# Expert keys of a product-key router: two one-hots over 16 ranks instead of one over 50 candidates, with the ranks stepped out on GpSimd

## The chip, the cores and the metric

The kernel runs on one core of a Trainium2 chip. The metric is the device time of one launch in microseconds. The engines are named as in the profile: PE (TensorE matmuls) and PEld (its weight loads), DVE (VectorE), ACT (ScalarE), POOL (GpSimd) and SP (SyncE, here only a queue of transfers). Each engine works through its own queue in order and waits on semaphores of the others.

## The reference, cut to what matters

Two layers, each a gated merge of four token mixers and then a PEER layer: a feed-forward layer whose 16384 experts per layer are found by product keys. 512 tokens of width 1024. The mixers are untouched by the change. What the router computes:

```python
def peer_ffn(h, w_query, sub_keys, expert_u, expert_v):
    q = (ht @ w_query).reshape(t, PEER_HEADS, 2, PEER_HALF).astype(f32)      # 8 heads, 2 halves
    sc = jnp.einsum("thpd,pkd->thpk", q, sub_keys.astype(f32))               # 128 keys per half
    s_top, i_top = lax.top_k(sc, PEER_TOPK)                                  # 16 best of each half
    cand = (s_top[:, :, 0, :, None] + s_top[:, :, 1, None, :]).reshape(t, PEER_HEADS, 256)
    best, pos = lax.top_k(cand, PEER_TOPK)                                   # 16 best pairs
    idx = (jnp.take_along_axis(i_top[:, :, 0, :], pos // PEER_TOPK, axis=-1) * PEER_KEYS
           + jnp.take_along_axis(i_top[:, :, 1, :], pos % PEER_TOPK, axis=-1))
    gate = jax.nn.softmax(best, axis=-1).astype(h.dtype)
    # then, chunk by chunk: gelu(expert_u[idx] . h) * gate, times expert_v[idx], summed
```

## The kernel before

**The work of a PEER layer.** All experts are computed densely for three of the four token tiles (384 tokens), and by gathered rows for the fourth. `up` (one call is a *block* here) multiplies 128 experts with the tokens: a block is 24 matmuls of 128x384, in three products of a split into a high and a low part. The weights of a block come by a transfer from SP (`wr`); ACT casts them (`wh`, line 108), DVE subtracts to get the low part (`wl`, line 109: the *split* below), PE multiplies. 92 blocks run in `up`, their results go to memory; the other blocks and the products with the second expert matrix follow in `Down`.

**The router** runs beside these blocks. `Router.pairs(t, R)` handles one token tile of 128 tokens: on DVE it sums the scores of the 50 rank pairs that can be among the best 16 (`cand`; the ranks of the first half from 0 to 7 have 16, 8, 5, 4, 3, 2, 2, 2 partners, ranks 8 to 15 one each: `ROWS`, `NCAND`), sums their keys in the same layout (`cidx`), takes the best 16 (`topk`, two calls of four heads), and turns the position of each winner (`posf`) into its key: per head, a one-hot of 16x50 on DVE (`eq`, line 1167), times `cidx` on POOL (line 1169), summed on DVE (line 1171). Last the key is parted into its two halves and the softmax is taken, with an Exp on ACT. `pairs` is called four times a layer: once for the gathered tile (`first`, beside blocks 2 to 12), then by `dense` for tiles 0, 1 and 2. After each of these three, `dense` transposes the result (`rT`), builds one-hots for 32 groups of four tokens (`oh`) and multiplies them on PE to a table of gates (`G`, `GB`). `gathered` gets rows of experts by indirect transfers that POOL issues (line 1251) and reduces them on DVE (`row`, line 1260), at 0.8 rows per block while `dense` runs.

**What sets the order.** The program is written out by hand. Each call of `bulk` first runs `Beside.tick`: every generator beside the blocks (`scores`, `pairs`, `dense`, `gathered`) gets a rate per block (`RF` 3.2 for the first `pairs`, `RG` 3.1 for `dense`) and goes on until the costs that it yields use that up. So a larger number at a `yield` spreads the work over more blocks. After the block's matmuls, `Stream.advance` issues the cast and the split for the block two further on. On DVE there stands therefore, block after block: the work beside, then one split. On ACT a cast stands behind the activation of the block before (line 1279), which waits for that block's matmuls. POOL holds the products of `pairs` and the indirect transfers in one queue.

The lines that matter here are 1145 to 1180 (`pairs`), 108 and 109 (`split`), 120 to 123 (the matmuls of a block) and 1251 and 1260 (`gathered`).

## Time and profile before

| | us |
|---|---|
| median of 3 runs | 4039.18 |
| lowest, highest | 4032.03, 4041.72 |
| the profiled execution | 4033.05 |
| span of its instructions | 4031.3 |
| busy: PE, PEld, DVE, ACT, POOL | 3877.6, 3363.8, 3217.4, 1477.9, 1697.8 |

The profile is of one execution. Busy time of PE is modelled, since matmuls overlap; where a weight load or a matmul stands with "<-DVE wl L109", PE had nothing to do until that split was done. Engine times in a timeline are start and duration, in us from the span's start; two instructions of DVE overlap by up to 0.1 us in it, so the distance from start to start is what an instruction costs its queue. The two layers follow each other: the blocks of `up` run from about 840 to 1345 and again from about 2840 to 3345.

### The profile page before, as it was taken

The page shows a single profiled execution, that of the slowest core. Times are in us where ns is not written, and L with a number is a line of the kernel's source. Part 1 is how long each engine was busy: PE and PEld are TensorE (multiplying, and loading weights), DVE is VectorE, ACT ScalarE, POOL GpSimd, SP SyncE. Part 2 cuts the span into 40 slices and gives each one's busy share as a digit, 9 for nine tenths or more (in the row PEclk, how much of TensorE's full clock was granted, in tenths as well). Part 3 has the DMA queues.
Part 4 walks back from the last instruction along what each step waited for, and adds up shares of the span by engine and source line. Part 5 has one row for each costly group of instructions (what it writes and reads, how often), then busy time and mean ns, then how long its engine had stood idle before and what let it go on. Part 6 is the DMA issues. An engine that isn't in the chain of part 4 may idle for free.

```text
span 4031.3 us, 56403 instructions
## 1 busy us (share of the span) xinstructions
PE 3877.6 (96%) x19994; PEld 3363.8 (83%) x19994; DVE 3217.4 (80%) x5869; ACT 1477.9 (37%) x2171; POOL 1697.8 (42%) x1566
## 2 busy tenths in 40 slices
PE   6899999999999999999988999999999999999998
PEld 5777777799999999888767777878999999998877
DVE  4667944799999777999857778448999997788997
ACT  4323233333444333333343232333344443333333
POOL 3410500024423566899743005000233326678995
PEclk9999999999999999999989999999999999999999
DMA  3322333346876899999923232333468768999997
GB/s 113 100 85 92 99 98 115 116 134 234 292 259 235 280 322 322 347 336 343 321 92 107 82 99 93 102 113 113 159 223 294 261 226 304 322 323 337 340 348 267
DMA packets 346650, 851.39 MB, mean 211 GB/s; under 512 B 43648, under 2 KB 164864, under 8 KB 342016
## 3 DMA queue, kind: packets, MB, share of 16 engines
q1 hardware_dynamic: 236048, 492.39, 36.7%
q0 software_dynamic: 74016, 272.66, 19.1%
q10 hardware_dynamic: 36304, 82.74, 5.7%
q8 instruction: 158, 2.59, 0.3%
q14 instruction: 124, 1.02, 0.1%
HBM read 754.60 MB, written 93.06 MB: 210 GB/s over the span
## 4 chain that ended last, share of the span: by engine, by line
PE 74%; DVE 13%; POOL 5%; issue 4%; DMA 3%; ACT 2%; SPq 0%; DVEq 0%; POOLq 0%; ACTq 0%
PE mm L120 14%; PE mm L123 13%; PE mm L122 13%; PE va L129 6%; PE va L132 6%; PE va L131 6%; PE G L1218 4%; DVE wl L109 3%; PE pb L120 2%; DMA as<-dS 1%; PE pb L123 1%; PE pb L122 1%; DVE row L1260 1%; DMA row<-in_v_dram,gidx 1%; POOL as L1322 1%
## 5 line engine op out<-in xcount | busy, mean ns | idle before, releaser
L109 DVE TENSOR_TENSOR wl<-wr,wh 128x1024 fp32r<-128x1024 f32 (+2 forms) x792 | 990.8, 1251 | 377.4 <-ACT wh L108 302.9
L123 PE MATMUL mm<-hl,wh 128*128 128x384 f32 (+1 forms) x3456 | 1235.9, 358 | 0.0
L122 PE MATMUL mm<-hh,wh 128*128 128x384 f32 (+1 forms) x3456 | 1235.8, 358 | 0.0
L108 ACT CAST wh<-wr 128x1024 fp32r<-128x1024 f32 (+2 forms) x792 | 789.0, 997 | 346.7 <-PE va L132 128.2
L120 PE MATMUL mm<-hh,wl 128*128 128x384 f32 (+1 forms) x3456 | 787.0, 370 | 46.2 <-DVE wl L109 42.4
L120 PEld LDWEIGHTS mm<-hh,wl 128*128 128x128 f32 x3456 | 619.8, 190 | 123.4 <-DVE wl L109 54.1
L122 PEld LDWEIGHTS mm<-hh,wh 128*128 128x128 f32 x3456 | 651.8, 189 | 56.8
L123 PEld LDWEIGHTS mm<-hl,wh 128*128 128x128 f32 x3456 | 651.1, 188 | 56.1
L1251 POOL DMA_INDIRECT row<-in_u_dram,gidx x256 | 389.4, 1521 | 611.1 <-DVE row L1260 561.7
L132 PE MATMUL va<-wh,al 128*128 128x512 f32 x1536 | 598.1, 389 | 0.8 <-DVE al L109 0.8
L131 PE MATMUL va<-wh,ah 128*128 128x512 f32 x1536 | 597.9, 389 | 0.0
L1169 POOL TENSOR_TENSOR eq<-eq,cidx 128x800 f32<-128x800 f32 x64 | 126.2, 1977 | 891.1 <-DVE eq L1167 885.4
L1251 POOL DMA_INDIRECT row<-in_v_dram,gidx x256 | 397.4, 1552 | 97.9 <-DVE gacc L1271 44.8
L1271 DVE SCALAR_TENSOR_TENSOR gacc<-row,z,gacc 128x1024 f32<-128x1024 f32 x254 | 413.3, 1627 | 20.4 <-DMA row<-in_v_dram,gidx 18.8
L129 PE MATMUL va<-wl,ah 128*128 128x512 f32 x1536 | 395.6, 392 | 7.3 <-DVE wl L109 7.2
L129 PEld LDWEIGHTS va<-wl,ah 128*128 128x128 f32 x1536 | 284.8, 188 | 70.3 <-issue 11.6
L1260 DVE SCALAR_TENSOR_TENSOR row<-row,h2row 128x1024 f32<-128x1024 f32 x256 | 339.3, 1335 | 1.6 <-DMA row<-in_u_dram,gidx 1.6
L132 PEld LDWEIGHTS va<-wh,al 128*128 128x128 f32 x1536 | 288.3, 188 | 62.2 <-DVE al L109 1.2
L131 PEld LDWEIGHTS va<-wh,ah 128*128 128x128 f32 x1536 | 288.3, 188 | 60.7
L108 ACT CAST ah<-as 128x384 fp32r<-128x384 f32 x256 | 131.0, 512 | 472.8 <-POOL as L1322 405.9
L109 DVE TENSOR_TENSOR al<-as,ah 128x384 fp32r<-128x384 f32 x256 | 173.0, 676 | 161.7 <-ACT ah L108 161.5
L1322 POOL TENSOR_TENSOR as<-as,GB 128x128 f32<-128x128 f32 x256 | 263.8, 1030 | 0.0
(345 smaller groups left out, 4331.8 us busy)
## 6 DMA issues: line engine op xcount, KB each, us to landing
wr<-in_uT_dram SPq DMA_DIRECT2D x256, 512.0 KB, 4.6
wr<-in_v_dram SPq DMA_DIRECT2D x256, 512.0 KB, 5.8
wr<-in_w_in_dram SPq DMA_DIRECT2D x144, 512.0 KB, 3.7
dS<-act ACTq DMA_DIRECT2D x184, 192.0 KB, 3.7
as<-dS SPq DMA_DIRECT2D x184, 192.0 KB, 6.7
dG<-GB ACTq DMA_DIRECT2D x32, 1024.0 KB, 6.7
ag<-dG SPq DMA_DIRECT2D x128, 256.0 KB, 6.7
wr<-in_w_query_dram SPq DMA_DIRECT2D x32, 512.0 KB, 3.7
```

Source lines behind the costliest of these rows:

```text
L108: e.nc.scalar.copy(hi, src)
L109: e.nc.vector.tensor_tensor(out=lo, in0=src, in1=hi, op=OP.subtract)
L120: e.nc.tensor.matmul(ps, al, bh, start=start and i == 0, stop=False)
L122: e.nc.tensor.matmul(ps, ah, bh, start=False, stop=False)
L123: e.nc.tensor.matmul(ps, ah, bl, start=False, stop=stop and i == n - 1)
L129: e.nc.tensor.matmul(ps, ah, bl, start=start, stop=False)
L131: e.nc.tensor.matmul(ps, ah, bh, start=False, stop=False)
L132: e.nc.tensor.matmul(ps, al, bh, start=False, stop=stop)
L1251: nc.gpsimd.indirect_dma_start(out=g, out_offset=None, in_=e.I["u" if n < 128 else "v"], in_offset=bass.IndirectOffsetOnAxis(ap=e.gidx[:, ...
L1260: V.scalar_tensor_tensor(g, g, 1.0, e.h2row, op0=OP.mult, op1=OP.mult, accum_out=z[:, k:k + 1])
L1271: V.scalar_tensor_tensor(e.gacc, g, z[:, k:k + 1], e.gacc, op0=OP.mult, op1=OP.add)
L1322: G.tensor_tensor(out=s[:, 4:6], in0=s[:, 4:6], in1=self.e.GB[:, :, (i + NS) % 128], op=OP.mult)
```

## The change

The keys of all 50 candidates (`cidx`) are no longer built. Instead, the position of a winner is turned into two ranks by 18 steps on POOL over 128x128 elements: `fo`, the first candidate of the winner's row (eight compare-and-scale steps over the row starts, added up), and `posf - fo`, the place in the row. Each rank is then looked up by a one-hot over 16 ranks for four heads at once: `eq` is now 4x16x16 = 1024 elements a partition, four of them per call instead of eight of 800, with product and sum on the same engines as before. The two halves of the key come out directly, so the parting at the end goes. The yields change with it: the lookups cost 4 x 1.2 and 2 x 2.4 times `CP` (1.4) instead of 4 x 1.0 and 6 x 1.9, the `cidx` yield of 1.2 x `CP` goes, and two yields of 2.0 stand between the 18 steps and the first one-hot. A call of `pairs` yields 28.7 in all instead of 34.5. A table of the row starts (`first`) is set up once at the start of the kernel.

```diff
@@ consts
+    e.first = p.tile([128, 16], F32, name="first")
+    for j in range(8):
+        nc.vector.memset(e.first[:, j:j + 1], float(sum(ROWS[:j])))
+    nc.vector.tensor_copy(e.first[:, 8:16], e.iota[:, NCAND - 8:NCAND])
@@ Router.pairs
-        ci = pb.tile([128, 8, NCAND], F32, name="cidx")
-        for dst, src in ((c, S1), (ci, I1)):
...
+        s = S1[:, t].rearrange("p (h q) k -> p h q k", q=2)
+        a0 = s[:, :, 0]
...
         V.tensor_copy(pf, pos)
-        idx = R[:, 3].rearrange("p (h k) -> p h k", k=16)
+        G = nc.gpsimd
+        fo, st = R[:, 0], R[:, 3]
+        pl = pf.rearrange("p h k -> p (h k)")
+        for j in range(1, 8):
+            G.tensor_scalar(st if j > 1 else fo, pl, float(sum(ROWS[:j])), float(ROWS[j - 1]), op0=OP.is_ge, op1=OP.mult)
+            if j > 1:
+                G.tensor_tensor(out=fo, in0=fo, in1=st, op=OP.add)
+        G.tensor_scalar(st, pl, float(NCAND - 8), None, op0=OP.is_ge)
+        G.tensor_scalar(R[:, 1], pl, float(sum(ROWS[:7])), None, op0=OP.subtract)
+        G.tensor_tensor(out=st, in0=st, in1=R[:, 1], op=OP.mult)
+        G.tensor_tensor(out=fo, in0=fo, in1=st, op=OP.add)
+        G.tensor_tensor(out=pl, in0=pl, in1=fo, op=OP.subtract)
+        yield 2.0
+        yield 2.0
+        rank = R[:, 0].rearrange("p (h k) -> p h k", k=16), pf
         eqs = {}
-        for h in range(10):
-            if h < 8:
-                eqs[h] = eq = self.pb.tile([128, 16, NCAND], F32, name="eq", tag="oh", bufs=OH)
-                V.tensor_tensor(out=eq, in0=bc(pf[:, h, :, None], [128, 16, NCAND]),
-                                in1=bc(e.iota[:, None, 0:NCAND], [128, 16, NCAND]), op=OP.is_equal)
-                nc.gpsimd.tensor_tensor(out=eq, in0=eq, in1=bc(ci[:, h, None, :], [128, 16, NCAND]), op=OP.mult)
-            if h > 1:
-                V.tensor_reduce(out=idx[:, h - 2], in_=eqs.pop(h - 2), axis=AX.X, op=OP.add)
-            yield (1.9 if 1 < h < 8 else 1.0) * CP
-        V.tensor_scalar(R[:, 0], R[:, 3], 1.0 / 128, -0.49609375, op0=OP.mult, op1=OP.add)
+        sh = [128, 4, 16, 16]
+        for i in range(6):
+            if i < 4:
+                q, h = i % 2, slice(i // 2 * 4, i // 2 * 4 + 4)
+                eqs[i] = eq = self.pb.tile(sh, F32, name="eq", tag="oh", bufs=OH)
+                tab = e.first if q == 0 else e.iota[:, 0:16]
+                V.tensor_tensor(out=eq, in0=bc(rank[q][:, h, :, None], sh), in1=bc(tab[:, None, None, :], sh),
+                                op=OP.is_equal)
+                key = I1[:, t].rearrange("p (h q) k -> p h q k", q=2)[:, h, q]
+                G.tensor_tensor(out=eq, in0=eq, in1=bc(key[:, :, None, :], sh), op=OP.mult)
+            if i > 1:
+                q, h = (i - 2) % 2, (i - 2) // 2 * 4
+                V.tensor_reduce(out=R[:, 1 if q else 3, h * 16:h * 16 + 64].rearrange("p (h k) -> p h k", k=16),
+                                in_=eqs.pop(i - 2), axis=AX.X, op=OP.add)
+            yield (2.4 if 1 < i < 4 else 1.2) * CP
+        V.tensor_copy(R[:, 0], R[:, 3])
...
-        V.tensor_scalar(R[:, 0], R[:, 0], 12582912.0, None, op0=OP.add)
-        V.tensor_scalar(R[:, 0], R[:, 0], 12582912.0, None, op0=OP.subtract)
-        V.scalar_tensor_tensor(R[:, 1], R[:, 0], -128.0, R[:, 3], op0=OP.mult, op1=OP.add)
+        if t == NT - 1:
+            V.scalar_tensor_tensor(R[:, 3], R[:, 0], 128.0, R[:, 1], op0=OP.mult, op1=OP.add)
```

DVE's queue in the call of `pairs` for tile 0 of layer 0, from the cast of the positions on, before the change (`wl` is a split, `row` a row of `gathered`):

```order
L1161 CAST posf<-pos 128x128
L1167 TENSOR_TENSOR eq<-posf,iota 128x800 x2
L1260 SCALAR_TENSOR_TENSOR row,z<-row,h2row 128x1024
L109 TENSOR_TENSOR wl<-wr,wh 128x1024
L1167 TENSOR_TENSOR eq<-posf,iota 128x800
L1171 TENSOR_REDUCE R<-eq 128x16
L109 TENSOR_TENSOR wl<-wr,wh 128x1024
```

The same place after the change, down to the first sum; `R` holds the first rank, `first` and `iota` are the tables it is compared with:

```order
L1161 CAST posf<-pos 128x128
L1281 SCALAR_TENSOR_TENSOR row,z<-row,h2row 128x1024
L114 TENSOR_TENSOR wl<-wr,wh 128x1024
L1281 SCALAR_TENSOR_TENSOR row,z<-row,h2row 128x1024
L114 TENSOR_TENSOR wl<-wr,wh 128x1024
L1185 TENSOR_TENSOR eq<-R,first 128x1024
L1185 TENSOR_TENSOR eq<-posf,iota 128x1024
L114 TENSOR_TENSOR wl<-wr,wh 128x1024
L1185 TENSOR_TENSOR eq<-R,first 128x1024
L1191 TENSOR_REDUCE R<-eq 128x64
L1281 SCALAR_TENSOR_TENSOR row,z<-row,h2row 128x1024
L114 TENSOR_TENSOR wl<-wr,wh 128x1024
```

Two blocks' worth of other work now stands between the cast and the first one-hot, which waits for POOL, and four splits stand beside the one-hots instead of seven. POOL's queue at that place, before:

```order
L1251 DMA row<-in_u_dram,gidx 128x1024 x5
L1169 TENSOR_TENSOR eq<-eq,cidx 128x800 x2
L1251 DMA row<-in_u_dram,gidx 128x1024
L1169 TENSOR_TENSOR eq<-eq,cidx 128x800 x2
L1251 DMA row<-in_u_dram,gidx 128x1024
```

POOL's queue there after the change, from the last of the steps on (the others stand ahead of these, one after the other):

```order
L1170 TENSOR_SCALAR R<-posf 128x128
L1171 TENSOR_SCALAR R<-posf 128x128
L1172 TENSOR_TENSOR R<-R 128x128
L1173 TENSOR_TENSOR R<-R 128x128
L1174 TENSOR_TENSOR posf<-posf,R 128x128
L1272 DMA row<-in_u_dram,gidx 128x1024 x2
L1188 TENSOR_TENSOR eq<-eq,I_5833 128x1024 x3
L1272 DMA row<-in_u_dram,gidx 128x1024
L1188 TENSOR_TENSOR eq<-eq,I_5833 128x1024
```

The 18 steps come first, then two indirect transfers, then the four products.

## Rows read from the trace of the kernel before

**Rows 1.** Waits of PE, 840 to 1260 (layer 0): who, us, times, longest.

```profile
PE mm L120 <- DVE wl L109: 16.3, 16, 3.3
```

**Rows 2.** Waits of PE, 2840 to 3260 (layer 1).

```profile
PE mm L120 <- DVE wl L109: 17.2, 16, 3.3
```

**Rows 3.** Timeline of PE, first matmuls of some blocks: start, us, what [idle before].

```profile
866.53 1.59 PE L120 MATMUL mm<-hh,wl 128*128 128x384 f32 x8
...
1058.16 1.55 PE L120 MATMUL mm<-hh,wl 128*128 128x384 f32 x8
1062.32 1.55 PE L120 MATMUL mm<-hh,wl 128*128 128x384 f32 x8
```

**Rows 4.** Timeline of DVE in the first call of pairs, layer 0.

```profile
854.45 0.98 DVE L1150 TENSOR_TENSOR cand<-S 128x128 f32<-128x128 f32 x8
...
855.49 0.22 DVE L1146 TENSOR_SCALAR i<-I 128x128 f32<-128x128 f32 x1
...
856.79 1.22 DVE L109 TENSOR_TENSOR wl<-wr,wh 128x1024 fp32r<-128x1024 f32 x1
857.92 0.54 DVE L1086 MAX8 best<-cand 128x8 f32<-128x50 f32 x4
...
860.99 1.20 DVE L109 TENSOR_TENSOR wl<-wr,wh 128x1024 fp32r<-128x1024 f32 x1
...
865.17 1.19 DVE L109 TENSOR_TENSOR wl<-wr,wh 128x1024 fp32r<-128x1024 f32 x1
866.30 0.21 DVE L1161 CAST posf<-pos 128x128 f32<-128x128 uint32 x1
```

**Rows 5.** Timeline of DVE in the call for tile 0, layer 0.

```profile
915.64 1.89 DVE L1167 TENSOR_TENSOR eq<-posf,iota 128x800 f32<-128x800 f32 x2
917.45 2.79 DVE L1260 SCALAR_TENSOR_TENSOR row<-row,h2row 128x1024 f32<-128x1024 f32 x1
...
920.17 2.76 DVE L109 TENSOR_TENSOR wl<-wr,wh 128x1024 fp32r<-128x1024 f32 x1
922.85 0.98 DVE L1167 TENSOR_TENSOR eq<-posf,iota 128x800 f32<-128x800 f32 x1
923.75 0.97 DVE L1171 TENSOR_REDUCE R<-eq 128x16 f32<-128x800 f32 x1
924.65 2.17 DVE L109 TENSOR_TENSOR wl<-wr,wh 128x1024 fp32r<-128x1024 f32 x1
```

**Rows 6.** Timeline of POOL at the same time.

```profile
916.78 5.06 POOL L1169 TENSOR_TENSOR eq<-eq,cidx 128x800 f32<-128x800 f32 x2 [5.83 <-DVE eq L1167]
...
923.98 1.76 POOL L1169 TENSOR_TENSOR eq<-eq,cidx 128x800 f32<-128x800 f32 x1 [0.19 <-DVE eq L1167]
```

**Rows 7.** Timeline of ACT: activation of a block, then the next cast.

```profile
1058.36 0.49 ACT L1279 ACTIVATE act<-mm 128x384 f32<-128x384 f32 x1 [2.16 <-PE mm L123]
1059.31 1.05 ACT L108 CAST wh<-wr 128x1024 fp32r<-128x1024 f32 x1 [0.45 <-ACT act L1279]
```

**Rows 8.** Timeline of POOL: dependent steps of 16 elements, DVE idle.

```profile
75.93 0.20 POOL L349 TENSOR_SCALAR s<-s 128x16 f32<-128x16 f32 x1
76.21 0.22 POOL L340 TENSOR_TENSOR s<-s,h 128x16 f32<-128x16 f32 x1
76.52 0.20 POOL L349 TENSOR_SCALAR s<-s 128x16 f32<-128x16 f32 x1
```

**Rows 9.** Timeline of POOL: two instructions of 128 elements, neither held up.

```profile
893.85 0.24 POOL L1194 IOTA iota<- 128x128 f32 x1
...
1407.06 0.46 POOL L1322 TENSOR_TENSOR as<-as,GB 128x128 f32<-128x128 f32 x1
```

**Rows 10.** Groups by line and shape: POOL, 128 elements, DVE busy (mean ns).

```profile
L587 POOL TENSOR_TENSOR VS<-VS,vsc 128x128 f32<-128x128 f32 x14 | 11.1, 790 | 1.1
```

**Rows 11.** Timeline of DVE, end of the first call of pairs.

```profile
898.16 0.21 DVE L1177 TENSOR_SCALAR R<-R 128x128 f32<-128x128 f32 x1
...
898.88 0.28 DVE L1182 TENSOR_REDUCE gsum<-R 128x8 f32<-128x128 f32 x1
```

More of the change, by code (lines that the diff above doesn't have):

```diff
@@ L1139, in pairs @@
         c = pb.tile([128, 8, NCAND], F32, name="cand")
-        ci = pb.tile([128, 8, NCAND], F32, name="cidx")
-        for dst, src in ((c, S1), (ci, I1)):
-            s = src[:, t].rearrange("p (h q) k -> p h q k", q=2)
-            a0 = s[:, :, 0]
-            if src is I1:
-                a0 = pb.tile([128, 8, 16], F32, name="i128")
-                V.tensor_scalar(a0, s[:, :, 0], 128.0, None, op0=OP.mult)
-            o = 0
-            for j in range(8):
-                n = ROWS[j]
-                V.tensor_tensor(out=dst[:, :, o:o + n], in0=s[:, :, 1, 0:n], in1=bc(a0[:, :, j:j + 1], [128, 8, n]),
-                                op=OP.add)
-                o += n
-            V.tensor_tensor(out=dst[:, :, o:o + 8], in0=a0[:, :, 8:16], in1=bc(s[:, :, 1, 0:1], [128, 8, 8]), op=OP.add)
-            yield 1.2 * CP
+        s = S1[:, t].rearrange("p (h q) k -> p h q k", q=2)
+        a0 = s[:, :, 0]
+        o = 0
+        for j in range(8):
+            n = ROWS[j]
+            V.tensor_tensor(out=c[:, :, o:o + n], in0=s[:, :, 1, 0:n], in1=bc(a0[:, :, j:j + 1], [128, 8, n]),
+                            op=OP.add)
+            o += n
+        V.tensor_tensor(out=c[:, :, o:o + 8], in0=a0[:, :, 8:16], in1=bc(s[:, :, 1, 0:1], [128, 8, 8]), op=OP.add)
+        yield 1.2 * CP
         best = pb.tile([128, 8, 16], F32, name="best")
```

## The prediction, made before the changed kernel was run

> **What bounds the kernel now.** I read the waits of PE first, stage by stage. Where the router's calls of `pairs` run, PE waits for one thing, the split on DVE: 16.3 us in layer 0 and 17.2 us in layer 1 [rows 1, 2], 16 times each and up to 3.3 us long. With 33.5 us in all out of 4031.3, this is what the change can win or lose; elsewhere in the `up` stage PE has no gap, and other stages are not touched. By the 16 block starts of PE's timeline that name the split as releaser, the 16.3 us of layer 0 are 3.6 in the first call, 6.7 in tile 0, 2.3 in tile 1 and 3.7 in tile 2.
>
> Next, why the split is late. A block takes PE 4.16 us [rows 3]. Behind a block come its activation, the next cast and then the split that goes with it; the cast ends 2.0 us after the block [rows 7], the split 1.14 later, and its own block stands two blocks on. So a split is at best done 5.1 us before it is needed: this is the most DVE can fall behind, and I call what is left of it at the cast of the positions the *head start*. In the first call it is almost used up: the split of 865.17 ends at 866.3 and its block starts at 866.53 [rows 3, 4].
>
> Last, what DVE and POOL do to each other. A two-input instruction of DVE and an instruction of POOL take turns and never run together. Read [rows 5, 6] side by side: POOL's first product of 800 waits until the second compare is done, then `row` (1.14 alone) needs 2.79, then the second product waits for `row`, and the split needs 2.76. Two products with 0.67 and 1.03 of such waits in them took 5.06, so one holds DVE up for 1.68. The sum over a one-hot is not held up: 0.97 beside the product of 923.98, while the split behind it needed 2.17.
>
> **The change part by part.**
>
> *Taken away.* Per call DVE loses `cidx` (855.49 to 856.79: 1.30 us [rows 4]), four of eight compares and sums (0.90 each from start to start [rows 5], now longer) and three small steps at the end (898.16 to 898.88: 0.72 [rows 11]). Compares and sums: 8 x 1.8 = 14.4 us before, 4 x (1.14 + 1.14) = 9.1 after, since 1024 elements cost a split's 1.13 to 1.14 [rows 4]. POOL's products go from 8 x 1.68 to 4 x 2.15 (1.68 x 1024/800).
>
> *Added: the 18 steps on POOL.* The first compare waits for the first 17 (the second rank for the 18th). No row shows them, so I bound the price. Below: dependent steps of 16 elements start 0.28 to 0.31 apart, of which 0.08 to 0.09 is the gap [rows 8]; 17 x 0.30 = 5.1 us. Above: all 17 as two-input steps of 128 elements, 0.45 + 0.09 = 0.54 [rows 9], 9.2 us. I take 0.54 for the eight two-input steps and, for the nine with one input, 0.30 + 0.08: between the step of 16 elements (0.20) and the two-input step, near the iota of 128 (0.24 [rows 9]). That is 4.3 + 3.4 = 7.7 us. The Trainium skill (GPSIMD Engine Reference, section 4.1 Engine selection) puts GpSimd at about line rate with one input and at half of VectorE's speed with two; by that estimate the one-input steps would cost as the iota, 0.24 + 0.09, the 17 steps 7.3 us, and the forecast below would be 4 us less (8 x 0.45). Each two-input instruction of DVE that falls into the steps pushes them back by about 1 us. In the first call and tile 1 two of these stand before the first compare (two splits; a `row` and a split), in tiles 0 and 2 four. So from the cast of the positions the ranks are ready after 0.2 + 7.7 + 2 = 10.0 us (rounded), or 11.8 us.
>
> DVE is at the first compare much sooner: two splits later, or 4 x 1.14, even paced by the casts after some 4 to 6 us. It then stands still. Behind the compare in its queue are the next splits, and PE waits for those. Behind the steps in POOL's queue are indirect transfers; these run three rows ahead at 0.8 rows per block, some 15 us, so that delay is covered.
>
> *Moved closer.* `pairs` now yields 28.7 instead of 34.5, and the one-hots stand beside four blocks instead of seven or so. From ranks ready to the last late split, DVE's queue holds four compares (4.6), three splits (3.4), two sums (2.3), and is held up by two products in full (4.3) and by two others for what a sum beside them leaves (2 x 1.0): 16.6 us, plus 2 x 1.14 for two `row` in the calls of `dense`. The remaining sums and the tail fit into the blocks behind.
>
> *Head starts.* First call: 0.2 + 1.3 from `cidx` = 1.5. In `dense` the queue starts from 5.1, as the blocks before are light: the call before ends earlier in units, and two or three blocks carry a split alone. A `topk` takes 3.07 and `cand` 1.04 [rows 4]; a block with `cand`, `topk` and split costs 5.2, one with `topk`, `row` and split 5.35, against 4.16. Tile 0 has both in a row: 5.1 - 1.1 - 1.2 = 2.8. Tiles 1 and 2 have a light block between: 3.9.
>
> *The sum per call* is ranks ready + queue - head start - blocks passed (five; four in tile 1, where one split less stands ahead):
> - first: 10.0 + 16.6 - 1.5 - 20.8 = 4.3 (before 3.6)
> - tile 0: 11.8 + 18.9 - 2.8 - 20.8 = 7.1 (6.7)
> - tile 1: 10.0 + 18.9 - 3.9 - 16.6 = 8.4 (2.3)
> - tile 2: 11.8 + 18.9 - 3.9 - 20.8 = 6.0 (3.7)
>
> That is 25.8 us of waits per layer. Before it was 16.3 and 17.2, in the mean 16.75; so +9.0. The three steps off the tail give back 0.7, as the transposes wait for it in places. Two layers: 2 x 8.3 = **+16.6 us**.
>
> *Costs nothing:* the eight memsets and the copy for `first`, ahead of the first layer's work, where DVE waits for the tokens (nine instructions of at most 0.2, under 2 us if nothing hid them); PE's matmuls, which are the same; the rows of `gathered`, whose rate per block is unchanged, so that `dense` ending some five blocks earlier moves no other work.
>
> Against the profiled execution, 4033.05 (span 4031.3 and 1.75 around it), this is 4049.7. That execution lies 6.1 under the median of 4039.18, within the spread of three runs; on the median's scale it is **4056**.
>
> **The rivals.** 0.3% of the kernel, about what a measurement can tell from no change, is 12 us.
>
> 1. *Cheap steps: a wash.* If a step costs what one of 16 elements does (0.30), the ranks come 2.6 us sooner in all eight calls: 16.6 - 20.8 = -4, so 4035. For it: a two-input step grows only from 0.22 to 0.46 over eight times the elements [rows 8, 9], so much of it is fixed, and one with a single input may hardly grow. Against: the 0.46 itself.
>
> 2. *The wait is covered, and it gets faster.* If the ranks are there when DVE comes (after about 5, 6, 3.5 and 6 us, by its own queue and the pace of the casts), the waits are 0, 1.3, 1.9 and 0.2 us: 3.4 per layer, so 2 x (3.4 - 16.75 - 0.7) = -28, 4011. The place is the first compare of each call. The point from which it is faster than before is a step of 0.33 on average instead of 0.45 (8.3 us per layer over four calls is 2.1 off 7.7, over 17 steps); for over 12 us it takes 0.24 (3.6 off), under every row of steps that I have. For it: the saved compares, sums, `cidx` and tail (7.3 us a call) are certain, and the two yields of 2.0 let one or two blocks pass. Against: DVE has no idle time before any of [rows 4, 5], so it reaches the compare by its queue and not at the blocks' pace.
>
> 3. *Steps at the busy price.* If the steps of 128 elements take 0.79 as they do beside a DVE full of two-input work [rows 10], 17 come to 15.0 with the gaps; that has the pushes in it, so it stands against my 9.7 and 11.5 and is some 4.3 us later: 34 more, 4090. Against: DVE stands still at the compare, so most steps run alone.
>
> 4. *Turns fall otherwise.* The products hold DVE up only where two-input work is next. If all four meet sums, 2.3 us a call go: 16.6 - 18 = -2, 4037; if all four hold up a split in full, it is +18, 4074.
>
> **How the numbers follow.** The forecast with steps between 0.38 and 0.54 and turns as counted, 4042 to 4068 (17 x 0.07 or 0.09 x 8 to either side): 0.55. Rival 1: 0.17. Rival 2: 0.11. Rival 3: 0.08. Rival 4: 0.09, half on each side. Slower by over 0.3% (over 4051): 0.38 of the forecast, rival 3 and half of rival 4, 0.50. Faster by over 0.3% (under 4027): rival 2 and the lower end of rival 1, 0.14. Within: 0.36. The range reaches from the middle between rivals 2 and 1 to the lower part of rival 3, and leaves out what is beyond: 4019 to 4084.
>
> **What would show it.** In the profile after: POOL's 18 steps in 8 to 12 us from the cast to the last; DVE idle for 4 to 7 us in front of the first compare, ended by POOL; the waits of PE for the split rising to about 26 us a layer, tile 1 the worst; products of 1024 near 2.2 us. Wrong, if DVE has no such idle time (rival 2), if steps take 0.3 (rival 1) or stay near 0.8 with DVE idle (rival 3), or if PE's waits fall though DVE idles: then my count of the queue after the ranks is too long.

## The result: 1.2% slower, and the profile after

| us | before | after |
|---|---|---|
| median | 4035.61 (4 runs) | 4083.26 (4 runs) |
| lowest, highest | 4027.64, 4041.72 | 4079.75, 4087.05 |
| the profiled execution | 4033.05 | 4087.05 |
| span of its instructions | 4031.3 | 4085.1 |

After stands to before as 1.0117 (95% interval 1.0103 to 1.0131): 47.6 us slower, where 16.6 was forecast. The direction was right, the size short by a factor of almost three.

Busy times of the changed kernel, from its page:

```profile
PE 3900.3 (95%) x19994; PEld 3387.2 (83%) x19994; DVE 3137.0 (77%) x5712; ACT 1478.3 (36%) x2171; POOL 1743.0 (43%) x1678
```

DVE has 80 us less to do, as the change wants, and the kernel is slower. PE does the same matmuls in 22.7 us more.

Where the time went is seen by the transfer that ACT issues behind each block of `up`. The first and the last of the 92 in layer 0 (start, us, what) stand so before:

```profile
845.46 0.33 ACTq L1280 DMA_DIRECT2D dS<-act  x1
...
1337.51 0.33 ACTq L1280 DMA_DIRECT2D dS<-act  x1
```

and after:

```profile
847.36 0.33 ACTq L1301 DMA_DIRECT2D dS<-act  x1
...
1362.42 0.33 ACTq L1301 DMA_DIRECT2D dS<-act  x1
```

That is 492.0 us before and 515.1 after, +23.0; in layer 1 it is 493.0 and 516.2, +23.2. Together that is 46.2 of the 53.8 us between the two profiled executions. The other 7.6 lie ahead of the two stretches, between them and behind them (1.9, 1.3 and 4.5), in stages that the change does not touch; the last of these alone takes from 687.6 to 700.5 us over all traces here. I call this stretch of layer 0 *`up`* below; all runs are compared by it too, since it leaves the spread of the other stages out.

The waits of PE in the two stretches, which answer to [rows 1, 2] (who, us, times, longest):

```profile
PE mm L125 <- DVE wl L114: 32.7, 11, 6.8
...
PE mm L125 <- DVE wl L114: 31.7, 11, 5.9
```

From 33.5 to 64.4 us (+30.9): fewer waits, but up to 6.8 us long instead of 3.3. The waits of DVE in layer 0 name what is behind them:

```profile
DVE eq L1185 <- POOL R L1173: 33.4, 4, 9.7
```

DVE stands still for 8.3 us on average in front of the first compare of each of the four calls. The first call on DVE, which answers to [rows 4] (start, us, operation, idle before and who ended it):

```profile
865.89 0.24 DVE L1161 CAST posf<-pos 128x128 f32<-128x128 uint32 x1
866.02 1.24 DVE L114 TENSOR_TENSOR wl<-wr,wh 128x1024 fp32r<-128x1024 f32 x1
868.35 1.23 DVE L114 TENSOR_TENSOR wl<-wr,wh 128x1024 fp32r<-128x1024 f32 x1 [1.09 <-ACT wh L113]
878.50 1.23 DVE L1185 TENSOR_TENSOR eq<-R,first 128x1024 f32<-128x1024 f32 x1 [8.93 <-POOL R L1173]
880.08 3.35 DVE L1185 TENSOR_TENSOR eq<-posf,iota 128x1024 f32<-128x1024 f32 x1 [0.35 <-POOL posf L1174]
883.35 1.21 DVE L114 TENSOR_TENSOR wl<-wr,wh 128x1024 fp32r<-128x1024 f32 x1
...
887.80 1.21 DVE L1191 TENSOR_REDUCE R<-eq 128x64 f32<-128x1024 f32 x1
888.93 2.57 DVE L114 TENSOR_TENSOR wl<-wr,wh 128x1024 fp32r<-128x1024 f32 x1
```

and POOL at the same time (answers to [rows 6]):

```profile
866.45 2.03 POOL L1167 TENSOR_SCALAR R<-posf 128x128 f32<-128x128 f32 x2 [389.44 <-PE mm L128]
868.56 1.33 POOL L1169 TENSOR_TENSOR R<-R 128x128 f32<-128x128 f32 x1
869.99 0.64 POOL L1167 TENSOR_SCALAR R<-posf 128x128 f32<-128x128 f32 x1
870.71 0.46 POOL L1169 TENSOR_TENSOR R<-R 128x128 f32<-128x128 f32 x1
871.26 0.64 POOL L1167 TENSOR_SCALAR R<-posf 128x128 f32<-128x128 f32 x1
...
876.35 0.53 POOL L1170 TENSOR_SCALAR R<-posf 128x128 f32<-128x128 f32 x1
...
878.01 0.46 POOL L1173 TENSOR_TENSOR R<-R 128x128 f32<-128x128 f32 x1
878.55 1.49 POOL L1174 TENSOR_TENSOR posf<-posf,R 128x128 f32<-128x128 f32 x1
```

Read both together: the cast of the positions is at 865.89, the 17th step ends at 878.47, the first compare starts at 878.50. Two splits are all that DVE has to do in between. The split that PE needs next stands behind two compares in DVE's queue and starts at 883.35.

What PE makes of it, the first matmuls of three blocks:

```profile
874.48 1.55 PE L125 MATMUL mm<-hh,wl 128*128 128x384 f32 x8
884.62 2.93 PE L125 MATMUL mm<-hh,wl 128*128 128x384 f32 x8 [5.82 <-DVE wl L114]
891.70 1.55 PE L125 MATMUL mm<-hh,wl 128*128 128x384 f32 x8
```

and PE's granted clock in windows of 5 us (PE, PEld, DVE, ACT, POOL busy, then clock, DMA share, GB/s):

```profile
880.00:885.00 5.00, 0.38 (x1) 0.38 (x2) 4.92 (x3) 0.83 (x1) 3.75 (x3) 0.89 0.11 39
885.00:890.00 5.00, 5.00 (x17) 5.00 (x17) 5.00 (x3) 0.00 (x0) 3.75 (x2) 0.50 0.32 105
890.00:895.00 5.00, 5.00 (x28) 5.00 (x27) 5.00 (x4) 1.55 (x2) 2.61 (x2) 0.92 0.46 139
```

After 5.82 us without work PE is granted 0.50 of its clock, the lower of its two levels (1.2 instead of 2.4 GHz), and the block takes 7.08 us from start to start instead of 4.16. Of the 22.7 us that PE is busy for longer, 18.1 stand in the two stretches of `up` (966.8 against 948.7), where such blocks are. The prediction had nothing on this, and whether it is a part of the loss had to be tried.

### The profile page after: what moved, and what is told of

Its sections match the earlier page's. It is cut to its first block, busy times and chain, and to the rows that moved or that the text cites. A ratio compares the mean times of both kernels' runs of the same rounds, so it can differ in the third digit from the quotient of the medians.

```text
span 4085.1 us, 56355 instructions
## 1 busy us (share of the span) xinstructions
PE 3900.3 (95%) x19994; PEld 3387.2 (83%) x19994; DVE 3137.0 (77%) x5712; ACT 1478.3 (36%) x2171; POOL 1743.0 (43%) x1678
## 4 chain that ended last, share of the span: by engine, by line
PE 72%; DVE 10%; POOL 8%; issue 4%; DMA 4%; ACT 1%; SPq 0%; DVEq 0%; POOLq 0%; ACTq 0%
PE mm L125 14%; PE mm L127 13%; PE mm L128 13%; PE va L134 5%; PE va L137 5%; PE va L136 5%; PE G L1239 4%; DVE wl L114 3%; DMA row<-in_v_dram,gidx 2%; DMA as<-dS 2%; PE pb L125 1%; PE pb L128 1%; PE pb L127 1%; POOL row L1272 1%; POOL R L1167 1%
## 5 line engine op out<-in xcount | busy, mean ns | idle before, releaser
L114 DVE TENSOR_TENSOR wl<-wr,wh 128x1024 fp32r<-128x1024 f32 (+2 forms) x792 | 980.3, 1238 | 416.6 <-ACT wh L113 339.6
L125 PE MATMUL mm<-hh,wl 128*128 128x384 f32 (+1 forms) x3456 | 802.6, 375 | 76.7 <-DVE wl L114 72.1
L125 PEld LDWEIGHTS mm<-hh,wl 128*128 128x128 f32 x3456 | 634.9, 194 | 151.6 <-DVE wl L114 81.2
L1272 POOL DMA_INDIRECT row<-in_v_dram,gidx x256 | 386.4, 1509 | 97.4 <-DVE gacc L1292 45.3
L1167 POOL TENSOR_SCALAR R<-posf 128x128 f32<-128x128 f32 x56 | 48.8, 871 | 834.4 <-PE mm L128 779.3
L134 PEld LDWEIGHTS va<-wl,ah 128*128 128x128 f32 x1536 | 284.2, 188 | 75.5 <-issue 16.3
L1281 DVE SCALAR_TENSOR_TENSOR row<-row,h2row 128x1024 f32<-128x1024 f32 x256 | 325.4, 1281 | 1.1 <-DMA row<-in_u_dram,gidx 0.8
```

The costliest lines, as they stand in the source:

```text
L114: e.nc.vector.tensor_tensor(out=lo, in0=src, in1=hi, op=OP.subtract)
L125: e.nc.tensor.matmul(ps, al, bh, start=start and i == 0, stop=False)
L134: e.nc.tensor.matmul(ps, ah, bl, start=start, stop=False)
L1272: nc.gpsimd.indirect_dma_start(out=g, out_offset=None, in_=e.I["u" if n < 128 else "v"], in_offset=bass.IndirectOffsetOnAxis(ap=e.gidx[:, ...
L1281: V.scalar_tensor_tensor(g, g, 1.0, e.h2row, op0=OP.mult, op1=OP.mult, accum_out=z[:, k:k + 1])
```

## The experiments

Two theories at the start. *The chain*: DVE's idle time in front of the first compare, made by 18 steps on POOL that are dearer than assumed, is the loss; the lower clock may add to it. *The packing*: the one-hots stand beside fewer blocks than before, and DVE falls behind for that reason.

| run | median, us | ratio to before (95%) | `up`, us | DVE idle before the first compares, us | PE waits for the split, us |
|---|---|---|---|---|---|
| before | 4035.6 | | 492.0 | 0 | 16.3 |
| after | 4083.3 | 1.0117 (1.0103 to 1.0131) | 515.1 | 33.4 | 32.7 |
| ranks on DVE | 4037.8 | 0.9997 (0.9983 to 1.0012) | 493.8 | 0 | 16.7 |
| no steps | 4005.3 | 0.9926 (0.9901 to 0.9950) | 478.9 | 0 | 7.6 |
| yields before the one-hots | 4055.9 | 1.0052 (1.0028 to 1.0076) | 502.0 | 12.8 | 27.0 |
| yields between the one-hots | 4070.4 | 1.0079 (1.0051 to 1.0107) | 509.3 | 32.0 | 30.4 |
| low part last | 4088.4 | 1.0113 (1.0086 to 1.0139) | 518.5 | 33.3 | 32.4 |
| half the steps | 4040.8 | 0.9991 (0.9976 to 1.0007) | 496.4 | 13.8 | 18.2 |
| matmuls in the waits | 4083.5 | 1.0108 (1.0082 to 1.0133) | 514.8 | 32.5 | 19.5 |
| ranks on DVE, wider | 4029.0 | 0.9989 (0.9976 to 1.0002) | 487.4 | 0 | 17.6 |
| ranks from the one-hots | 4029.3 | 0.9980 (0.9971 to 0.9990) | 490.2 | 0 | 14.6 |
| the same, wider | 4026.1 | 0.9973 (0.9964 to 0.9983) | 488.4 | 0 | 13.3 |
| more steps | 4123.5 | 1.0211 (1.0194 to 1.0228) | 538.0 | 56.3 | 54.2 |

The last three columns are of layer 0 in the profiled execution. Not all runs were on the same chip (the kernel before had medians from 4035.6 to 4041.3 beside them), so ratios are compared. One value of `up` is good to some 3 us: run 9, which has the kernel before behind a row of extra instructions, has 495.4 where the kernel before has 492.0.

**1. The ranks on DVE.**

```diff
-        G = nc.gpsimd
+        G = nc.vector
         fo, st = R[:, 0], R[:, 3]
```

(The products stay on GpSimd.)

> The 18 steps for the ranks are issued on DVE in place of GpSimd, nothing else is changed. Theory 1 (the chain of steps): the changed kernel loses because DVE stands still for 8.3 us in front of the first compare of each call, and PE's granted clock falls after the long waits that follow. On DVE a step of 128 elements should cost about 0.2 to 0.25 from start to start (the cast of the positions takes 0.22), 18 of them some 4.5 us, without the idle time: PE's waits for the split fall from 32 to about 14 us a layer, the stretches at the lower clock go, 4030 (4015 to 4045). Theory 2 (the packing): the one-hots now stand beside four blocks in place of seven and their products of 1024 elements hold DVE up; then DVE has 4.5 us of work more per call in the same place, the waits stay over 25 us a layer and the time over 4060.

DVE in the first call:

```profile
861.74 0.24 DVE L1161 CAST posf<-pos 128x128 f32<-128x128 uint32 x1
862.02 0.37 DVE L1167 TENSOR_SCALAR R<-posf 128x128 f32<-128x128 f32 x2
862.42 0.29 DVE L1169 TENSOR_TENSOR R<-R 128x128 f32<-128x128 f32 x1
...
866.73 0.29 DVE L1174 TENSOR_TENSOR posf<-posf,R 128x128 f32<-128x128 f32 x1
```

From the cast to the next split DVE's queue needs 5.2 us for the 18 steps, where the changed kernel has 12.6 us from the cast to the first compare, 8.9 of them idle; and the kernel is level with the one before, with the same one-hots in the same places. So the packing alone does not make the loss; where the steps stand does.

**2. No steps.**

```diff
-        for j in range(1, 8):
-            ...
-        G.tensor_tensor(out=pl, in0=pl, in1=fo, op=OP.subtract)
...
-        rank = R[:, 0].rearrange("p (h k) -> p h k", k=16), pf
+        rank = pf, pf
```

> The 18 steps are left out: both one-hots are taken from the positions as they are, so the keys are not the right ones; all else stands as in the changed kernel. This prices the steps by themselves. Theory 1: no DVE idle time ended by POOL before a compare, PE's waits under 8 us a layer, no stretch at the lower clock, 4000 to 4020, so that the steps cost 65 to 80 us. Theory 2: the one-hots are as close together as before, waits over 25 us a layer, above 4050.

PE's waits in layer 0:

```profile
PE mm L125 <- DVE wl L114: 7.6, 6, 1.9
```

All else of the change is worth 0.74%, and the 18 steps take back 1.9%. From the cast to the first compare DVE needs 3.6, 6.0, 3.0 and 6.5 us for its own splits in the four calls: so much of a chain is hidden.

**3 and 4. More room ahead of the one-hots, or among them.** The same six units of yield in two places:

```diff
-        yield 2.0
-        yield 2.0
+        yield 5.0
+        yield 5.0
```

> The two yields between the steps and the one-hots are 5.0 each in place of 2.0, six units or some 2 blocks (8 us) more, in which DVE has splits to do while POOL does the steps. Theory 1: DVE's idle time before the first compare falls from 8.3 to under 3 us, PE's waits to some 10 us a layer, 4005 to 4030. Theory 2: the one-hots are as close together as they were, waits over 25 us, above 4050.

```diff
-            yield (2.4 if 1 < i < 4 else 1.2) * CP
+            yield (2.4 if 1 < i < 4 else 1.2) * CP + 1.0
```

> The same six units as in the run with the longer yields ahead of the one-hots, but put between the one-hots: each of their six yields is 1.0 longer. Theory 1: DVE's idle time before the first compare stays at 8.3 us, the first long wait of each call stays and with it the lower clock behind it; only the later waits shrink: 4060 to 4075. Theory 2: the one-hots stand beside six blocks, nearly as before the change, and the time goes back to about 4035.

Room among the one-hots leaves the idle time at 32.0 us and gains little, as the chain has it. Room ahead of them cuts it to 12.8, but gains 13 us of `up` where some 30 were expected: my number failed, and the packing's number (above 4050) was met for another reason, which the trace shows. DVE's waits in layer 0 with the room ahead:

```profile
DVE eq L1185 <- POOL R L1173: 12.8, 4, 3.8
DVE row L1281 <- DMA row<-in_u_dram,gidx: 9.5, 2, 5.2
```

and POOL in the call for tile 0:

```profile
917.34 1.50 POOL L1167 TENSOR_SCALAR R<-posf 128x128 f32<-128x128 f32 x1
918.92 0.46 POOL L1169 TENSOR_TENSOR R<-R 128x128 f32<-128x128 f32 x1
919.47 0.64 POOL L1167 TENSOR_SCALAR R<-posf 128x128 f32<-128x128 f32 x1
920.19 1.51 POOL L1169 TENSOR_TENSOR R<-R 128x128 f32<-128x128 f32 x1
...
931.09 2.00 POOL L1272 DMA_INDIRECT row<-in_u_dram,gidx  x1 [0.16 <-issue]
```

The splits that were to hide the chain hold it up: a step that meets a split takes 1.50 instead of 0.64 or 0.46, and the chain, 12.6 to 13.7 us from cast to first compare in the changed kernel, takes 14.1 to 16.3 here. And the indirect transfers behind the steps in POOL's queue now come too late: DVE waits 9.5 us for `row`. Work put beside this chain is paid for twice.

**5. The low part last.** Each block of `up` does the products with `wl` last instead of first:

```diff
+            e.nc.tensor.matmul(ps, ah, bh, start=start and i == 0, stop=False)
+            e.nc.tensor.matmul(ps, ah, bl, start=False, stop=False)
+        for i, (ah, al, bh, bl) in enumerate(pairs):
+            e.nc.tensor.matmul(ps, al, bh, start=False, stop=stop and i == n - 1)
```

> The changed kernel, with the products of a block in `up` in another order: the eight that need the split (`wl`) come last in place of first, so each block can start 16 matmuls or 2.6 us before its split is there. This tests the sum of the prediction, in which a call's waits are one backlog (ranks ready + queue - head start - blocks): with 2.6 us more head start per call, each of the eight calls loses 2.6 us of waits, 64 to some 43 us, and with the waits shorter a part of the stretches at the lower clock goes, 5 to 15 us: 4050 (4043 to 4058). Rival: every wait is a delay of its own and shrinks by 2.6, 64 to 23 us, with nearly all of the lower clock gone: about 4022. Second rival: PE then waits for something else just as long (the cast on ACT): no change, 4083.

Nothing was gained. DVE's waits in layer 0 show a wait that the changed kernel does not have:

```profile
DVE wl L114 <- issue: 22.7, 12, 4.9
...
DVE wl L114 <- PE mm L129: 6.4, 3, 3.3
```

There are two buffers of `wl`. The block reads its low part 2.6 us later, and so the buffer comes free 2.6 us later: the need and the earliest start of the split both moved, and the head start grew by no more than 0.5 us (5.6 at most instead of 5.1, by the end of the block and 1.14 for the split). A third buffer would be the clean form; it was not tried. So this run says nothing against the sum by head starts, and nothing for it.

**6 and 7. Half the steps, and half as many again.**

```diff
-        for j in range(1, 8):
+        for j in range(1, 6):
             ...
-        G.tensor_scalar(st, pl, float(NCAND - 8), None, op0=OP.is_ge)
-        ...
```

> Only the first 9 of the 18 steps are done, the rest is left out, so the ranks are not the right ones; all else stands as in the changed kernel. The chain on GpSimd should take about 6.5 us in place of 12.6. If its price is proportional (every us of it delays a split): halfway between the run without steps (4005) and the changed kernel (4083), 4045. If the first 5 us or so are hidden, because DVE has splits of its own to do there, as the prediction's second rival has it: 4005 to 4025, with DVE idle for under 2 us before the first compare.

```diff
-        for j in range(1, 8):
+        for j in [1, 2, 3, 4, 5] + list(range(1, 8)):
```

> The changed kernel with the first nine of the 18 steps done twice (the result is the same), so that the chain is 5.8 us longer (five steps of one input at 0.72 from start to start, four of two inputs at 0.55). From the runs without steps, with half of them and with all, `up` takes 478.9, 496.4 and 515.1 us in layer 0 at chains of 0, about 8.3 and 13.1 us: the first 4 us or so are hidden behind DVE's own work and each us beyond costs about 1.0 us in each of four calls. If that holds, `up` takes 515.1 + 4 x 5.8 = 538 us in layer 0 and the kernel 46 us more than the changed one, about 4130 (4118 to 4140). If part of a longer chain is hidden again by blocks that pass, or if PE's lower clock adds to it: under 4110, or over 4145.

DVE's wait for the ranks in layer 0, with half the steps:

```profile
DVE eq L1180 <- POOL R L1169: 13.8, 4, 4.9
```

and with more:

```profile
DVE eq L1185 <- POOL R L1173: 56.3, 4, 15.4
```

The chain of nine steps took 7.9 to 9.1 us, not 6.5, since splits and `row`s fell into it; the ratio puts the run at 4032 beside a kernel before of 4035.6, between the 4005 to 4025 of a hidden chain and the proportional 4045. A part of the chain is hidden behind DVE's own splits, and the rest is paid for. Four runs with the same one-hots now stand side by side: idle time of 0, 13.8, 33.4 and 56.3 us against `up` of 478.9, 496.4, 515.1 and 538.0. The last three lie on a line: each microsecond in which DVE stands still costs 41.6/42.5, that is 0.98 us (0.99 in layer 1). The run without steps lies 4 us under that line; why is not shown. The last point was forecast from the other three as 538 and came out at 538.0; that it fits to the tenth is luck, since one value is good to some 3 us, but the 23 us over the changed kernel are well clear of that. The kernel's time, forecast as 4118 to 4140, was 4123.5. This is what settles the cause.

**8. Matmuls in the waits.** Does the lower clock add to the loss?

```diff
+        nw = WARM.get(key[2], 0) if key[0] == "u" else 0
+        for i in range(nw):
+            e.nc.tensor.matmul(pw, e.hh[:, i % KD, 0:128], e.hh[:, i % KD, 0:n], start=True, stop=True)
```

(`WARM` gives 10 to 25 for seven blocks of each layer.)

> The changed kernel with extra matmuls on PE (128x384, results not used), 10 to 25 of them ahead of the seven blocks per layer that wait longest for their split, 2 to 4.3 us each, about three quarters of each wait. Theory 1 (the lower clock after a long wait is a cost of its own, some 22 us): the splits come no sooner, but the blocks behind run at the higher clock, 4.2 us in place of 6 to 7, and the time falls by 15 to 25 us to about 4062, though PE does 40 us more work. Rival (the long block is long because its split or the next one is late, and the clock has no part in it): 4083, or slower by what sticks out of the waits.

PE around the block that had waited 5.82 us:

```profile
872.44 4.50 PE L321 MATMUL warm<-hh 128*128 128x384 f32 x25
878.48 1.66 PE L128 MATMUL mm<-hh,wl 128*128 128x384 f32 x8 [1.54 <-DVE wl L117]
885.43 1.96 PE L128 MATMUL mm<-hh,wl 128*128 128x384 f32 x8 [2.51 <-DVE wl L117]
```

and its clock there:

```profile
876.00:881.00 5.00, 3.46 (x20) 3.14 (x19) 5.00 (x3) 0.00 (x0) 3.42 (x2) 1.00 0.31 97
881.00:886.00 5.00, 2.49 (x15) 2.17 (x14) 5.00 (x4) 1.53 (x2) 2.37 (x1) 1.00 0.13 48
```

The clock holds 1.00, the block runs at its full pace, and then PE waits 2.51 us for the next split: 6.95 us to the next block instead of 7.08. The time is the same, where theory 1 had 15 to 25 us less. It falls in this point: while DVE is behind, the slow block only fills time in which the next split is not there yet, and waits and slow blocks are two faces of one delay, which DVE's queue sets.

That the lower clock costs nothing at all is not shown. Here too it fell behind the next wait (0.71, and that block took 5.86 us where the changed kernel has 4.64 at 1.00), while the block behind the last long wait of tile 1 ran in 4.18 us instead of 5.83: the level time is a balance of such blocks. And two executions of the kernel before, that of the top and that of run 9, show what it costs where DVE has caught up. The same block, after the same wait:

```profile
883.35 1.66 PE L120 MATMUL mm<-hh,wl 128*128 128x384 f32 x8 [2.21 <-DVE wl L109]
...
971.66 2.51 PE L147 MATMUL mm<-hh,wl 128*128 128x384 f32 x8 [2.21 <-DVE wl L136]
```

From start to start the block takes 4.27 us at a granted clock of 1.00 in the first and 5.84 at 0.71 in the second, no wait follows in the rest of the call, and the 1.6 us do not come back. With a like block in tile 0 this is the 3.4 us between the two values of `up`, at the same waits (16.3 and 15.9).

**9. What the steps cost alone.** Dependent steps, four of each form, at the start of the kernel before.

```diff
+    for n in (16, 64, 128, 256, 512):
+        a, b = pa[:, 0:n], pb_[:, 0:n]
+        for r in range(4):
+            G.tensor_scalar(a, a, 1.0, None, op0=OP.mult)
...
+            G.tensor_scalar(a, a, 0.5, 1.0, op0=OP.is_ge, op1=OP.mult)
...
+            G.tensor_scalar(a, a, 1.0, 0.0, op0=OP.mult, op1=OP.add)
```

> The kernel before, with a row of dependent instructions put at its start, on GpSimd and on DVE by turns, four of each form, over 16, 64, 128, 256 and 512 elements: one input with one operation (mult, is_ge), one input with two operations (is_ge and mult, mult and add), two inputs (mult, add). It prices the steps with nothing beside them. If the prediction's price were right (one input 0.30, two inputs 0.46 at 128), the 0.53 and 0.64 of the changed kernel would come from something beside them; theory 1 says that they are what these forms cost alone: 0.53, 0.64 and 0.46 at 128 elements, and 0.21 and 0.29 on DVE.

Groups by line and shape over the first 120 us (busy, mean ns of one); line 102 is `is_ge`, 104 `is_ge` and `mult`, 106 `mult` and `add`, 108 two inputs, 112 on DVE `is_ge` and `mult`, 114 on DVE two inputs:

```profile
L108 POOL TENSOR_TENSOR pa<-pa,pb 128x512 f32<-128x512 f32 x4 | 5.0, 1262 | 0.3
...
L114 DVE TENSOR_TENSOR pa<-pa,pb 128x512 f32<-128x512 f32 x4 | 2.8, 692 | 0.1
L104 POOL TENSOR_SCALAR pa<-pa 128x128 f32<-128x128 f32 x4 | 2.6, 643 | 0.3
...
L102 POOL TENSOR_SCALAR pa<-pa 128x128 f32<-128x128 f32 x4 | 2.1, 529 | 0.3
...
L108 POOL TENSOR_TENSOR pa<-pa,pb 128x128 f32<-128x128 f32 x4 | 1.8, 455 | 0.3
...
L106 POOL TENSOR_SCALAR pa<-pa 128x128 f32<-128x128 f32 x4 | 1.2, 301 | 0.3
...
L106 POOL TENSOR_SCALAR pa<-pa 128x16 f32<-128x16 f32 x4 | 0.8, 204 | 0.3
```

The prices of the changed kernel are what the forms cost with nothing beside them. The one-input step of [rows 8] has 0.20 us at 16 elements, and here `mult` and `add` has 0.204, `is_ge` and `mult` 0.274: that row is a `mult` and `add`, as the kernel's calls of that helper (`ts(s, s, ..., 1.0, OP.mult, OP.add)`) say too. At 128 elements this form costs 0.301, the price that I had put on all one-input steps; the steps of the change are `is_ge` forms, at 0.529 and 0.643.

**10 to 12. Versions that might win.** With the chain out of the way, what is left is DVE's own queue. First the ranks on DVE with a yield in the middle of the steps and wider one-hots:

```diff
+        yield 2.0
         G.tensor_scalar(st, pl, float(NCAND - 8), None, op0=OP.is_ge)
...
-            yield (2.4 if 1 < i < 4 else 1.2) * CP
+            yield (2.4 if 1 < i < 4 else 1.2) * CP + 1.0
```

> The ranks on DVE (18 steps, 5.2 us a call), one yield of 2.0 put in the middle of them, and each of the six yields of the one-hots 1.0 longer. What is left of PE's waits in the run with the ranks on DVE is 33.5 us, from DVE's own queue. Theory 1 (DVE's queue decides once no chain is waited for; more blocks beside it let it catch up): waits fall to about 20 us, 4018 to 4030 against 4036 for the kernel before. Rival (blocks gained are lost again behind): within 5 us of the kernel before.

4029.0, ratio 0.9989: `up` is 4.6 us shorter than before in layer 0, and the gain over the kernel before is not certain. PE's waits (17.6) are no shorter than in run 1, where theory 1 had them fall by some 40%; but none is over 2.2 us long, PE's clock in `up` is 1.00 instead of 0.99, and its busy time there is 7.0 us shorter (469.8 against 476.9), which is the gain over run 1 (6.3).

Then a form that needs no chain of steps. The first compare asks `is_ge` against the first positions of the 16 ranks, and the keys are replaced by their differences, so that the sum over the ranks passed gives the key itself; with 128 times the differences of the first positions added in, the same sum gives the first position too:

```diff
+        G.tensor_tensor(out=dk[:, :, 1:16], in0=kk[:, :, 0, 1:16], in1=kk[:, :, 0, 0:15], op=OP.subtract)
+        G.tensor_tensor(out=dk[:, :, 1:16], in0=dk[:, :, 1:16], in1=bc(self.df[:, None, 1:16], [128, 8, 15]), op=OP.add)
...
+                V.tensor_tensor(out=eq, in0=bc(pf[:, h, :, None], sh), in1=bc(tab[:, None, None, :], sh),
+                                op=OP.is_equal if q else OP.is_ge)
+                key = kk[:, h, 1] if q else dk[:, h]
```

> The ranks are got from the one-hots themselves: the first compare is `is_ge` against the first positions of the 16 ranks, and the product is with differences of neighbouring keys plus 128 times those of the first positions, so its sum is the first key plus 128 times the first position of its rank; five steps of 64 elements on DVE part the two and give the second rank, and only then comes the second one-hot. GpSimd has two steps of 120 elements left, which stand ahead of the top 16. Theory 1: what costs is the chain of steps that is waited for; without it the time lies between the run without steps (4005) and that with the ranks on DVE (4038): DVE has 10 short steps or some 1.7 us a call more than without steps, 4010 to 4020. Rival: the second one-hot now waits for the sum of the first, a chain of its own through GpSimd's product (2.4 us) and back, some 3 us a call: 4030 or more, with DVE idle before the sums.

4029.3, ratio 0.9980: faster than before, but outside my 4010 to 4020. The rival's reason is not it either: in layer 0 DVE waits 1.2 us in all for a sum over the first one-hot. `up` is 11.3 us longer than without steps, of which I had given 6.8 to the ten short steps on DVE; the rest was not found.

The same with the yields set anew:

```diff
-        yield 2.0
         yield 2.0
...
-            yield (2.4 if 1 < i < 4 else 1.2) * CP
+            yield (2.6 if 1 < i < 4 else 1.7) * CP
```

> The same as the run that gets the ranks from the one-hots, with one yield of 2.0 ahead of the one-hots in place of two, and 0.7 more at the first and last two and 0.28 more at the middle two yields of the one-hots, so that the splits stand more evenly between them. Theory 1: the waits that are left (some 15 to 20 us) shrink by a third, 4003 to 4015. Rival: no change against the run without this.

4026.1, not the 4003 to 4015 that were expected: the waits shrank from 14.6 to 13.3 us only. The ratio of 0.9973 (0.9964 to 0.9983) makes it 0.27% faster than the kernel before and 1.4% faster than the changed one, the fastest of those that do the whole computation. Against the run above, the two intervals overlap, so the rival (no change) stands.

## Why the prediction was right in direction and short in size

**What bounds.** Right as to the place: the calls of `pairs` carry the loss (46.2 of 53.8 us between the profiled executions), through the split. But the sum took lost time for PE's waits alone. These grew by 30.9 us; PE's longer work in the two stretches is another 18.1, and its other waits there, 2.9 us before, are gone.

**What the removed work is worth.** Right. The second rival's sum for a covered wait is `up` of 492.0 - 16.75 + 3.4 - 0.7 = 478 us; without steps it was 478.9. In its parts the agreement is luck: PE still waits 7.6 us where that sum has 3.4, and its busy time in `up` fell by 3.1 us (474.3 to 471.2), which the sum does not have. That rival's mechanism is real, but its condition, a step of 0.33, is not met on GpSimd.

**The price of a step: the term that failed.** Two-input steps were right (0.55 from start to start against 0.54). One-input steps were taken as 0.38 from start to start and cost 0.72 (seven) and about 0.56 (two, 1.12 together). The 17 steps alone come to 8 x 0.55 + 5.04 + 1.12 = 10.6 us, not 7.7. From cast to first compare it was 12.6, 13.5, 12.7 and 13.7 us where 10.0, 11.8, 10.0 and 11.8 stood: 8.9 us more in layer 0 and 8.7 in layer 1, **17.6 of the 29.6 us** that `up` is over the forecast (46.2 - 16.6). The price alone is more than that, 2.9 us a call or 23 in all; the pushes by DVE's instructions, taken as 2 us in two calls and 4 in the others, came to 1.5 to 1.8 and 2.6 to 2.7 in layer 0 and gave some of it back. The row that I took it from was of another operation; the prediction looked at its shape and its number of inputs and not at what it computes. The bound above (0.54 for all steps, 9.2 us) was wrong with it: two inputs are not dearer than one with these operations.

The Trainium skill (GPSIMD Engine Reference, section 4.1 Engine selection) would have had it cheaper still, 4 us below the forecast. On two inputs the runs come near it: 1.262 against 0.692 us over 512 elements, 1.8 times VectorE. On one input they do not: `is_ge` and `mult` takes 1.923 us over 512 elements against 0.427 on VectorE, and of the forms that were run only `mult` and `add` is cheaper than two inputs. The measurement decides.

**The queue behind the ranks and the head starts.** With the measured chains my sum gives waits of 34.7 us a layer and `up` of 509.2; it was 515.1. The 5.9 us that are missing stand for the most part in the first call, which took 11.5 us over the blocks' pace where the sum has 6.9: PE waits 1.66 us before the cast already, for a block that stands beside `cand` and the first `topk`, which are one yield closer than before (the run without steps has this wait too, so it is not the chain's); at the cast no head start is left (the split of 864.76 ends at 865.99, its block starts at 866.12) where the sum has 1.5; and from 878.50 to the last late split's end at 896.28 it is 17.8 us and not 16.6, with products of 2.34 to 2.40 alone, not 2.15. The remainder in tiles 0 to 2 was not taken apart.

**The turns.** As said: splits beside a product need 2.57, the sum beside one 1.21. The Trainium skill (SBUF — State Buffer, section Who interferes with whom) says that a DVE instruction with two inputs contends with a GpSimd instruction that reads, and that a sum along the row never does; these rows agree. The prediction had the pushes on the steps too, at 1 us each. What follows from them it did not see, and experiment 3 shows it: the steps cannot be hidden behind splits for nothing.

**The transfers behind the steps.** Right in the changed kernel (0.8 us of waits of DVE for `row` in the whole kernel, 1.6 before), and wrong where more blocks, and `row`s with them, go by beside the chain (experiment 3, 20.7 us). A longer chain alone does not do it: with more steps these waits are 2.0 us, since DVE stands still meanwhile.

**The clock.** Not foreseen, and PE's 22.7 us of longer work look like half of the loss. Experiment 8 says that while DVE is behind they are not a loss of their own; behind the last late split of a call they can be one, and how much of the 46.2 us that is was not measured.

**The signs that were named.** DVE's idle time was to be 4 to 7 us a call and was 8.9, 7.7, 9.7 and 7.1; the waits of PE were to be 25.8 us a layer with tile 1 the worst, and were 7.8, 9.3, 8.4 and 7.2, 32.7 in all: tile 1 as forecast (8.4), the other three longer. The 18 steps were to take 8 to 12 us and took 14.2 in the first call, the last of them beside a compare.

**The rivals.** The first (cheap steps) is out: no step is at 0.30. The third gave 4090 and is nearest in number, but not in its reason, since steps took 0.46 to 0.64 with DVE idle and not 0.79. The fourth is too small either way for what was seen. The time lies at the upper edge of the range (4083 of 4084), which was drawn that far for the third rival: that it holds is luck.

## What to carry to other kernels

Price a step by a row of the same operation on the same engine: the shape and the number of inputs don't fix it. A chain of short dependent steps on a slower engine, in front of an instruction of an in-order queue, costs its full length beyond what that queue has to do anyway; sum it first, and compare with what the same steps cost in the queue that waits (5.2 us from the cast on DVE against 12.6 on GpSimd here). Where waits come with a lower clock behind them, don't add the two up before a run has told them apart, and look whether the engine that is waited for has caught up behind them.

## What the runs showed of the hardware

- On GpSimd, over 128 fp32 elements: `is_ge` or `mult` by a constant 0.53 us, `is_ge` and `mult` 0.643, two inputs 0.455, but `mult` and `add` 0.301. From 128 to 512 elements each element costs 2.5, 3.3, 2.1 and 0.83 ns. The form with more arithmetic can be the cheapest.
- On DVE the `is_ge` and `mult` over 128 elements takes 0.227 us and two inputs 0.292.
- PE's granted clock fell to 0.50 in the 5 us that follow a wait of 5.82 us. With 25 matmuls put into that wait it stayed at 1.00 there, and fell to 0.66 in the 5 us behind the next wait, of 2.51 us. Behind a wait of 2.21 us at the same block it stayed at 1.00 in one execution of the kernel before and was 0.71 over the block in another.
